# Rescheduling the transform stage of a hybrid encoder layer: query weights, output gates, Fourier output and row-0 corrections

## The chip, the cores and the metric

The kernel runs on one core of a Trainium2 chip. The metric is the device time of one execution in microseconds, median of three runs. All work is for that core: five engines with queues of their own (PE for matmuls, VectorE or DVE, ScalarE or ACT, GpSimd or POOL, SyncE or SP, which here only issues DMAs). Each engine takes its instructions strictly in the order that was fixed when the program was built.

## The reference

Two sequences of 1024 tokens and 1024 channels go through one encoder layer and a final norm, all in fp32. What matters for the change:

```python
mod = silu(c) @ w_ada + b_ada                  # six vectors: sh1, sc1, ga1, sh2, sc2, ga2
h = rmsnorm(x, g_mix) * (1 + sc1) + sh1
z = h @ w_in                                   # 256 q_lat | 128 kv_lat | 64 k_pe | 512 f_in
q = rmsnorm(q_lat, g_q_lat) @ w_uq             # 4 heads of 128 + 64 (the 64 with rope)
kv = rmsnorm(kv_lat, g_kv_lat) @ w_ukv         # keys and values of 4 heads
y_mla = softmax(q k^T / sqrt(192)) v           # 512 wide
fr = real(fft2(f_in, over tokens and within 8 groups of 64 channels, ortho))
y_four = fr @ w_four                           # per group, 512 wide
x = x + ga1 * (concat(y_mla, y_four) @ w_out)
h2 = rmsnorm(x, g_ffn) * (1 + sc2) + sh2
x = x + ga2 * ((silu(h2 @ w_gate) * (h2 @ w_up)) @ w_down)
y = rmsnorm(x, g_final)
```

## The kernel before

**Products.** An fp32 product is made from three matmuls of a rounded format (`mm3`, L79 to L81): high by high, high by low, low by high. `split` (L62 to L64) makes the two parts of an operand: a cast of the high part on ScalarE (L63) and a subtract for the low part on VectorE (L64). So every operand of a matmul costs one instruction on each of these engines, and the matmul waits for both. A matmul of 512 columns fills one PSUM bank.

**Stages.** (1) To about 234 us: modulation vectors, then eight "pairs" k = 0 to 7 (four of each sequence; two row blocks each): norm, transposes, the input projection `zproj` (L400), the latents of queries and keys (`latents`, with their own norm: squares on ScalarE at L411 and L412, a chain of six small GpSimd instructions at L102 to L109, scaling on VectorE at L423 and L424, transposes on PE at L438), and the first half of the Fourier transform. Since a real transform has a symmetry over tokens, `evenodd` (L386) makes sums and differences of mirrored blocks on GpSimd (L397), splits them, and `fourier_in` (L445) multiplies them by the channel-side matrices; the results are summed in `zc` (cosines), `zs` (sines) and a row-0 tile `zx`. While pair 7 runs, SP loads the tables `tcos`, `tsin`, `tcor` and the first of the folded weights into eight staging tiles of one tag (`raw_tile`).

(2) 234 to 332 us, the transform stage. For each sequence `dft` (L784) multiplies by the token-side tables: even rows of cosines into `pe`, odd rows into `po`, with a correction by `tcor` and the row-0 tile `zx` (L795) in `pe`. `prep_wm` (L821) loads and splits the folded weights (Fourier weights times output weights: `wm_d`, and `wn_d` for the Nyquist rows). `fourier_out` (L855) takes, for one row block j, both column halves g: 6 matmuls and one of the Nyquist rows into `pa`, 6 into `pb`, then sum and difference of the two give two mirrored row blocks, which SP stores to `fo_d`. For j = 0 there are 7 more (row 0). Between the row blocks of sequence 0 stand the second modulation's products (`mod2`). In sequence 1, `gate_wo` (L882) loads the output weights in eight tiles, multiplies them by the gate `ga1` on GpSimd (L896) and stores them to `wog_d` from GpSimd's queue (L897). `stage3_loads` (L707) loads what the attention of sequence 0 needs, one DMA chained behind the other: latents, the queries' latents, the raw query weights into staging tiles, the rope tables, the key latents; it splits the query weights. The first block's queries are then projected (`rope_q`, `absorb_q`, `rope_flip`) between the last row blocks of the Fourier output.

(3) 332 to about 790 us: attention in 64 items k (sequence, block of 256 queries, head, half). One item: scores on PE (L1050 to L1054), maximum (L1059), exponential (ACT L1064), scaling (L1066) on VectorE, transposes on PE (L1078), splits, values. Other work is hung on items by a table `todo` (from L1127): `wv_load` (L1110) loads the output weights (at k = 0 the gated ones from `wog_d` for sequence 0, at k = 34 and 35 the raw ones for sequence 1, which are then gated on GpSimd, L1118), `wv_split` (L1121) splits them, one tile an item for k = 3 to 10; the output projection begins at k = 11.

(4) 790 us to the end: the feed-forward block as seven products of quarter matrices, with sums of quarters on GpSimd and VectorE that are stored to and reloaded from DRAM (in the gate and up stage GpSimd stores at L1370 and L1384 to L1399), and the final norm.

**What sets the order.** The program is written in order, and a scheduler of the framework places each instruction in its engine's queue by that order and by its inputs. `issue_after(x)` and `first(a, b)` add an order between two instructions without a wait at run time, `behind()` puts splits after the last ones made.

The order in a pair and the loop over the Fourier output, in two lines each:

```python
fourier_in(k, 0); latents(k, 1); fourier_in(k, 1)      # in pair(k), L602 on
evenodd(k + 1, here["p"])
...
for s in range(2):
    for j in (1, 2, 3, 0):
        fourier_out(s, abn, j)                         # both halves g; s == 0: mod2 twice
```

## Time and profile before

| | us |
|---|---|
| median of 3 runs | 2078.36 |
| the runs | 2078.17, 2082.8, 2078.36 |
| the profiled execution | 2084.17 |
| its span in the profile | 2082.4 |
| busy: PE, VectorE, ScalarE, GpSimd | 2023.8, 1415.4, 896.3, 822.6 |

The span is the stretch from the first to the last recorded instruction; the execution's own time has 1.8 us around it. In the timeline a row gives start, duration, engine, line, operation, the tiles written and read, partitions and columns, and in brackets how long the engine had been idle before it and which instruction ended that. Matmuls overlap: their rows start one after the other more closely than their durations say, so a matmul's price is the distance of two starts. A row of the waits gives the waiting engine, line and tile, what it waited for, total, times and longest. The granted clock is the share of full speed at which PE was allowed to run.

### The profile page before, as it was taken

Reading aid. Unit: us, or ns where it says so; the run is one execution under the profiler, and the core shown is the slowest. Engines: PE = TensorE matmul, PEld = TensorE weight load, DVE = VectorE, ACT = ScalarE, POOL = GpSimd, SP = SyncE. Lnnn points to the kernel's source line nnn. Section 1 sums busy time; section 2 is a strip of 40 time slices with the busy share of each in tenths; the row PEclk is TensorE's granted clock in tenths of the full one; section 3 lists DMA queues with packets and bytes.
Section 4 is the critical chain, followed back from the end, with each engine's and each line's share of the span. In section 5 each row is a group of like instructions: output and inputs, shape, how many; then the busy total and the mean of one; then the engine's idle time right before and its main releaser. Section 6 shows DMA issues by size and latency. Waiting matters only on the chain.

```text
span 2082.4 us, 28692 instructions
## 1 busy us (share of the span) xinstructions
PE 2023.8 (97%) x9994; PEld 1658.4 (80%) x9994; DVE 1415.4 (68%) x2095; ACT 896.3 (43%) x1749; POOL 822.6 (40%) x1014
## 2 busy tenths in 40 slices
PE   7799989999999999999999999999999999999998
PEld 4688858888888887888888888887788888888876
DVE  4567757766676669777677666778665565566675
ACT  2655535555565555233332356454323323336441
POOL 0554211111312316778778610333554454420142
PEclk9999999999999999999999999999999999999999
DMA  9685685544553466546455488665332232258662
GB/s 389 201 255 166 223 314 204 132 102 92 146 122 112 160 220 219 173 174 205 164 177 200 159 267 269 213 233 185 112 118 101 82 121 102 77 172 282 227 230 94
DMA packets 184909, 374.56 MB, mean 180 GB/s; under 512 B 18716, under 2 KB 58524, under 8 KB 181692
## 3 DMA queue, kind: packets, MB, share of 16 engines
q1 hardware_dynamic: 166780, 317.14, 44.9%
q0 software_dynamic: 17984, 55.59, 8.9%
q8 instruction: 78, 1.28, 0.2%
q14 instruction: 67, 0.55, 0.1%
HBM read 258.56 MB, written 122.49 MB: 183 GB/s over the span
## 4 chain that ended last, share of the span: by engine, by line
PE 53%; DVE 3%; DMA 3%; POOL 1%; issue 1%; ACT 1%; SPq 0%; DVEq 0%; ACTq 0%; POOLq 0%
PE bank L81 18%; PE bank L80 18%; PE bank L79 17%; DVE wl L64 1%; DVE val L138 1%; DMA draw<-t_d 1%; DMA val<-x_d 1%; POOL val L138 1%; DMA draw<-s_d 1%; DMA draw<-in_w_down_dram 0%; ACT wh L63 0%; DVE val L1606 0%; DVE val L135 0%; DMA X<-hc_d 0%; DMA ga<-ga_d 0%
## 5 line engine op out<-in xcount | busy, mean ns | idle before, releaser
L81 PE MATMUL bank<-H,wl 128*128 128x512 f32 x1232 | 490.6, 398 | 0.2 <-DVE wl L64 0.2
L79 PE MATMUL bank<-H,wh 128*128 128x512 f32 x1232 | 483.8, 393 | 3.0 <-DVE val L138 1.1
L80 PE MATMUL bank<-H,wh 128*128 128x512 f32 x1232 | 486.1, 395 | 0.3 <-DVE H L64 0.3
L79 PEld LDWEIGHTS bank<-H,wh 128*128 128x128 f32 x1232 | 231.2, 188 | 60.4 <-DVE val L138 2.0
L80 PEld LDWEIGHTS bank<-H,wh 128*128 128x128 f32 x1232 | 231.3, 188 | 59.9 <-DVE H L64 0.6
L81 PEld LDWEIGHTS bank<-H,wl 128*128 128x128 f32 x1232 | 231.3, 188 | 53.9 <-DVE wl L64 0.5
L64 DVE TENSOR_TENSOR wl<-draw,wh 128x512 fp32r<-128x512 f32 x286 | 201.7, 739 | 83.9 <-ACT wh L63 83.3
L138 DVE TENSOR_TENSOR val<-bank,val 128x512 f32<-128x512 f32 x200 | 136.5, 688 | 157.2 <-PE bank L81 150.2
L63 ACT CAST wh<-draw 128x512 fp32r<-128x512 f32 x286 | 168.5, 619 | 158.6 <-PE bank L80 83.4
L138 POOL TENSOR_TENSOR val<-val 128x512 f32<-128x512 f32 x58 | 84.0, 1457 | 365.0 <-DVE val L1580 188.7
L80 PE MATMUL bank<-wl,wh 128*128 128x512 f32 x572 | 223.7, 391 | 2.2 <-DVE wl L64 2.2
L63 ACT CAST wh<-rgu 128x512 fp32r<-128x512 f32 x172 | 106.8, 621 | 270.1 <-PE bank L80 211.0
L81 PE MATMUL bank<-wh,wl 128*128 128x512 f32 x572 | 222.7, 389 | 0.0
L79 PE MATMUL bank<-wh 128*128 128x512 f32 x572 | 222.6, 389 | 0.0
L63 ACT CAST wh<-val 128x512 fp32r<-128x512 f32 x133 | 82.1, 620 | 268.7 <-PE bank L80 249.2
L64 DVE TENSOR_TENSOR wl<-val,wh 128x512 fp32r<-128x512 f32 x133 | 131.9, 994 | 76.1 <-ACT wh L63 76.0
L64 DVE TENSOR_TENSOR wl<-rgu,wh 128x512 fp32r<-128x512 f32 x172 | 166.8, 970 | 4.9 <-ACT wh L63 4.9
L135 POOL TENSOR_TENSOR val<-rgu 128x512 f32<-128x512 f32 x80 | 118.5, 1481 | 102.6 <-DMA rgu<-in_wgu_dram 88.3
L80 PEld LDWEIGHTS bank<-wl,wh 128*128 128x128 f32 x572 | 107.4, 188 | 28.1 <-DVE wl L64 5.8
L79 PEld LDWEIGHTS bank<-wh 128*128 128x128 f32 x572 | 107.4, 188 | 22.5
L81 PEld LDWEIGHTS bank<-wh,wl 128*128 128x128 f32 x572 | 107.4, 188 | 22.0
L1059 DVE TENSOR_REDUCE mx<-ps_s 128x1 f32<-128x1024 f32 x64 | 78.2, 1222 | 63.7 <-PE ps_s L1054 63.5
(352 smaller groups left out, 4113.6 us busy)
## 6 DMA issues: line engine op xcount, KB each, us to landing
rgu<-in_wgu_dram SPq DMA_DIRECT2D x86, 512.0 KB
draw<-s_d SPq DMA_DIRECT2D x143, 256.0 KB
s_d<-val POOLq DMA_DIRECT2D x88, 256.0 KB, 3.9
draw<-t_d SPq DMA_DIRECT2D x88, 256.0 KB
s_d<-val SPq DMA_DIRECT2D x66, 256.0 KB
draw<-in_w_down_dram SPq DMA_DIRECT2D x55, 256.0 KB
wada<-in_w_ada_dram SPq DMA_DIRECT2D x11, 1024.0 KB
xt<-in_x_dram SPq DMA_DIRECT2D x16, 512.0 KB
```

Of the source, the lines that this page charges most:

```text
L63: here["a"] = nc.scalar.copy(hi, src).ins
L64: here["v"] = nc.vector.tensor_tensor(out=lo, in0=src, in1=rd(hi), op=ALU.subtract).ins
L79: nc.tensor.matmul(out, lh, rh, start=first, stop=False, skip_group_check=cont)
L80: nc.tensor.matmul(out, lh, rl, start=False, stop=False, skip_group_check=cont)
L81: here["t"] = nc.tensor.matmul(out, ll, rh, start=False, stop=last, skip_group_check=cont).ins
L135: return eng.tensor_tensor(out=out, in0=x, in1=y, op=ALU.subtract).ins
L138: eng.tensor_tensor(out=out, in0=x, in1=y, op=ALU.add)
L1059: nc.vector.tensor_reduce(out=mx, in_=ps, axis=AX.X, op=ALU.max)
```

## The change

- **Odd halves.** The casts of the differences of pairs 2 to 7 are ordered behind the squares of that pair's first projection on ScalarE; GpSimd's products keep their place.
- **Row-0 copies** (three small ones a sequence) go from VectorE to ScalarE.
- **Ahead of pair 7** come the split of the row-0 tile, the cast of `tcor`, the split of the cosines of sequence 0 and the first quarter of the folded weights (rows 0 and 1, left half). SP's order there is `tcos`, `tsin`, `tcor`, weights.
- **`dft`:** the corrections follow the odd products. The zeroing of the Nyquist tile goes from VectorE to GpSimd.
- **Folded weights by column halves:** own tiles for each half; `fourier_out` takes one half, and a sequence runs through t = 0 to 7: all j of the left half, then all j of the right. One `mod2` a step. The Nyquist weights' subtract and scaling go from VectorE to GpSimd.
- **Query weights:** one DMA loads them raw into the tile of their low part during sequence 0, and they are split in place at t = 4 and 6 of sequence 0.
- **`stage3_loads`** loads the queries' latents and the rope tables only; latents and key latents are issued behind the stores of t = 0 to 3 of sequence 1. `rope_q` stands at t = 3, `absorb_q` and `rope_flip` at t = 5.
- **Output gates:** `gate_wo` and `wog_d` go. At k = 0 the raw output weights are loaded and the gates; the eight multiplies on GpSimd stand two an item at k = 4 to 7, the splits two an item at k = 6 to 9.
- **The program's space for GpSimd's DMA descriptors** is 8192 bytes (the framework's default is 16384).

```diff
@@ evenodd, zproj, fourier_in
+                    if i == 1 and k > 1:
+                        st1.setdefault(("odd", k), []).append(here["a"])
...
+            if u == 0:
+                for ins in st1.pop(("odd", k), ()):
+                    first(here["sq"], ins)
...
-                    nc.vector.tensor_copy(zx[0:1, NCOS * s : NCOS * s + NCOS], pc[0:1, :NCOS])
+                    nc.scalar.copy(zx[0:1, NCOS * s : NCOS * s + NCOS], pc[0:1, :NCOS])
@@ ahead of pair(nk - 1)
+        nc.sync.dma_start(cor[:, :NTE], a["tcor"])
+        nc.scalar.copy(tcor, cor[:, :NTE])
+        split(zxs[0], zxs[1], zx)
+        z0 = zcos_split(0)
+        def wm_half(s, g, h, pool):
+            wm = [pool.tile([P, 2, 512], F32R, tag=f"wm{i}{g}{h}", name=f"wm{i}{g}{h}", bufs=1) for i in range(2)]
+            for c in range(2):
+                raw = raw_tile("wraw")[:, :512]
+                here["wraw"] = nc.sync.dma_start(raw, wm_d[s][:, 2 * h + c, 512 * g : 512 * g + 512]).ins
+                if h == 0:
+                    split(wm[0][:, c, :], wm[1][:, c, :], raw)
...
+        wm0 = wm_half(0, 0, 0, wr)
         pair(nk - 1)
@@ stage3_loads
-        last = gate_wo(0, gate_after, None)
+        for i in range(2):
+            last = nc.sync.dma_start(rd(ql[i]), lat_d[0][i][:, 0:2, 0:256]).ins
...
-        for c in range(2):
-            then(wqr[c][1][:, :256], wq_d[:, c, 512:768])
-            then(wqr[c][0], wq_d[:, c, 0:512])
...
+        S["ld2"] = [(rd(lat[i]), lat_d[0][i][:, 2:4, :]) for i in range(2)] + [(rd(ckv[i]), ckv_d[0][i]) for i in range(2)]
@@ transform stage
-        here["ny"] = nc.vector.tensor_scalar(out=nyt, in0=raws[0, 0], scalar1=0.0, scalar2=None, op0=ALU.mult).ins
+        nc.gpsimd.tensor_scalar(out=nyt, in0=raws[0, 0], scalar1=0.0, scalar2=None, op0=ALU.mult)
...
-                for i in range(2):
-                    nc.tensor.matmul(pe[:m, :NTE], zxs[i][:, x0 : x0 + m], tcor, start=False, stop=i == 1)
                 for c in range(2):
                     mm3(po[:m, :256], zz[0][:, 2 * c + 1, :], zz[1][:, 2 * c + 1, :],
                         tb[0][0][:, c, NTE:NT], tb[0][1][:, c, NTE:NT], c == 0, c == 1)
+                for i in range(2):
+                    nc.tensor.matmul(pe[:m, :NTE], zxs[i][:, x0 : x0 + m], tcor, start=False, stop=i == 1)
...
+                nc.gpsimd.tensor_tensor(out=wnr, in0=wnr, in1=rd(wnh), op=ALU.subtract)
+                nc.gpsimd.tensor_scalar(out=wnr, in0=wnr, scalar1=cmask[:, 3 + 2 * s : 4 + 2 * s], scalar2=None, op0=ALU.mult)
...
+        nyq_split()
+        zsplit(0, z0)
+        nc.sync.dma_start(rd(wq_l), wq_d)
...
-            for j in (1, 2, 3, 0):
-                with tc.issue_after(S.pop("ld")) if (s, j) == (1, 1) else ExitStack():
-                    fourier_out(s, abn, j)
-                if (s, j) == (1, 1):
-                    gate_wo(1, None, here["st"])
+            for t in range(8):
+                with tc.issue_after(S["ld"]) if s == 1 and t < 2 else ExitStack():
+                    fourier_out(s, abn, (1, 2, 3, 0)[t % 4], t // 4)
+                if s == 1 and t < 4:
+                    with tc.issue_after(here["st"]):
+                        nc.sync.dma_start(*S["ld2"].pop(0))
...
+                    if t in (4, 6):
+                        c = t // 2 - 2
+                        with behind():
+                            split(wq_h[:, c, :], wq_l[:, c, :], rd(wq_l[:, c, :]))
@@ attention
-                nc.sync.dma_start(raw, (wog_d if s == 0 else wo_d)[:, h, gs])
+                nc.sync.dma_start(raw, wo_d[:, h, gs])
...
+        def wv_gate(i):
+            h, g = i % 4, i // 4
+            with tc.issue_after(here["p"]):
+                nc.gpsimd.tensor_tensor(out=S["wv", h, g], in0=S["wv", h, g], in1=S["ga"], op=ALU.mult)
...
-            todo[3 + i].append(lambda i=i: wv_split(i))
+            todo[(4, 4, 5, 5, 6, 6, 7, 7)[i]].append(lambda i=i: wv_gate(i))
+            if i == 3:
+                todo[5].append(lambda: gate_half(0, 1))
+            todo[6 + i // 2].append(lambda i=i: wv_split(i))
@@ program
-    nc = _bacc.Bacc("TRN2", target_bir_lowering=False, num_devices=1)
+    nc = _bacc.Bacc("TRN2", target_bir_lowering=False, num_devices=1, dynamic_dma_scratch_size=8192)
```

194 lines of the change are left out of this document (77 added, 117 removed).

## The prediction

> **What bounds the kernel now.** First the page's first part, for the engine that fills the span.
>
> ```profile
> span 2082.4 us, 28692 instructions
> ...
> PE   2023.8 (97%) x9994; PEld 1658.4 (80%) x9994; DVE 1415.4 (68%) x2095; ACT 896.3 (43%) x1749; POOL 822.6 (40%) x1014
> ```
>
> TensorE is busy for all but 58.6 us, and the change keeps its number of matmuls. So it can win only idle time of TensorE in the stages that it touches, and time in which TensorE ran at a lower clock. The waits of the transform stage (230 to 330 us) show the largest one and what stood behind it; the PE timeline shows its place.
>
> ```profile
> PE bank L79 <- ACT wq_h L63: 7.5, 1, 7.5
> ACT wq_h L63 <- DMA wqr<-wq_d: 5.5, 2, 5.2
> ```
> ```profile
> 290.65 0.48 PE L79 MATMUL bank<-wm,A 128*128 128x512 f32 x1
> ...
> 292.36 0.50 PE L79 MATMUL bank<-wm,B 128*128 128x512 f32 x1 [0.53 <-ACT wm L847]
> ...
> 311.45 0.80 PE L79 MATMUL bank<-wq_h,ql 128*128 128x256 f32 x2 [7.53 <-ACT wq_h L63]
> ...
> 330.78 0.40 PE L79 MATMUL bank<-wm,A 128*2 128x512 f32 x1
> ...
> 332.41 0.39 PE L1050 MATMUL ps_s<-lat,qa 128*128 128x512 f32 x1
> ```
>
> The query projection of the first attention block waits for weights that are loaded and split only then; the matmuls of the Fourier output stand behind it in PE's queue. The stretches by window (columns: us, then PE, PEld, DVE, ACT, POOL busy, granted clock, DMA share, GB/s) show what such gaps cost on top.
>
> ```profile
> 206.00:212.00 6.00, 4.17 (x22) 3.89 (x21) 3.68 (x9) 4.83 (x14) 4.37 (x11) 0.72 0.10 26
> 239.30:242.30 3.00, 2.99 (x14) 2.81 (x15) 2.42 (x5) 1.49 (x4) 0.00 (x0) 0.50 0.45 143
> 247.30:290.30 43.00, 43.00 (x237) 28.42 (x236) 25.24 (x45) 13.11 (x27) 1.58 (x3) 1.00 0.83 299
> 304.00:311.40 7.40, 0.00 (x0) 0.00 (x0) 3.46 (x6) 0.99 (x2) 1.01 (x2) 0.71 1.05 397
> 311.40:317.20 5.80, 5.75 (x19) 5.08 (x20) 4.16 (x11) 3.44 (x6) 1.41 (x2) 0.50 0.96 354
> ```
>
> After the 7.53 us gap the clock is 0.50 for 5.8 us, and it was 0.50 for 3.0 us after a gap of 1.88 us at 239.31 (below). Between the two, 247.3 to 290.3, PE is never idle: nothing is to be had there, only lost.
>
> **The change part by part.**
>
> **A, the query weights** (loaded whole into the low part's own tile during sequence 0 and split there; the gate products of the output weights, their loads and stores gone from this stage; Fourier output by column halves). From 290.65 to 332.41 the stretch has 118 matmuls of 512 columns (8 row-and-column blocks of 13, and two times 7 for row 0), 18 of 256 columns and 8 transposes. From 330.78 to 332.41 are 7 intervals: 0.233 us for 512 columns; 256 columns go at 0.12 (below); a transpose at 0.13 (8 in 1.06 us, row at 550.63 below). Full: 118 x 0.233 + 18 x 0.12 + 8 x 0.13 = 30.7 us, against 41.8. The loss of 11.1 is 7.53 + 0.53 + 2.9 (half of 5.8 us at clock 0.50) and 0.1 rest. Is something late in its place? The weights are split behind the fifth and seventh step of sequence 0, near 270 us, some 30 us ahead of use. The latents (2 MB) and the key latents (1 MB) now stand on SP behind the stores of the first four steps of sequence 1, that is from about 294 to 304 us; 3 MB at the 354 GB/s of the row above are 8.9 us, so by about 313 to 316, before the first score, which would then stand at 332.4 - 10.5 = 321.9. Credit 10.5 (the 0.53 wait on a weight half may stay); bounds 7.6 (the clock still drops somewhere) and 11.1.
>
> **B, the start of the transform** (row-0 corrections behind the odd products, cosine splits, row-0 splits and the first weight half done in the last pair, the zeroing of the Nyquist tile and the Nyquist weights' subtract and scale moved from VectorE to GpSimd).
>
> ```profile
> 234.57 0.28 PE L79 MATMUL bank<-tb,zh 128*128 128x258 f32 x1
> ...
> 235.85 0.39 PE L81 MATMUL bank<-tb,zh 128*128 128x258 f32 x1 [0.88 <-DVE zh L64]
> ...
> 239.31 0.58 PE L795 MATMUL bank<-tcor,zx 128*128 128x258 f32 x1 [1.88 <-DVE zx L64]
> ...
> 246.10 0.28 PE L81 MATMUL bank<-tb,zh 128*128 128x256 f32 x1
> ...
> 247.30 0.39 PE L79 MATMUL bank<-wm,A 128*128 128x512 f32 x1
> ```
>
> From 246.10 to 247.30 are 10 intervals, so 0.12 each; the 66 matmuls from 234.57 on would take 7.9 us and took 12.73. Both operands that came late are now made earlier, and the corrections come after six more matmuls (0.7 us). Of the 4.8 us, 0.88 + 1.88 + 1.5 (3.0 us at clock 0.50) = 4.3 goes. What may be late next: the Nyquist and sine splits, which now head VectorE's queue, and the Nyquist weights, wanted by the seventh matmul of the Fourier output (1.4 us after its start) behind two GpSimd passes. No trace shows these; bounds 3.5 and 4.8, I take 4.3, the two rows' own.
>
> **C, the odd halves' casts.** These are the rows of pair 6, on ScalarE, GpSimd and PE.
>
> ```profile
> 202.81 0.62 ACT L63 CAST eoh<-eo 128x512 fp32r<-128x512 f32 x1 [7.04 <-POOL eo L397]
> ...
> 204.59 0.38 ACT L411 ACTIVATE junk<-bank 128x256 bf16<-128x256 f32 x1
> ```
> ```profile
> 201.49 2.54 POOL L397 TENSOR_TENSOR eo<-hf 128x512 f32<-128x512 f32 x2 [5.03 <-DVE eol L64]
> 205.40 0.22 POOL L102 TENSOR_SCALAR rs_v<-mz 128x2 f32<-128x2 f32 x1 [1.37 <-ACT junk L412]
> ...
> 207.32 0.20 POOL L109 TENSOR_TENSOR rs_r<-rs_w,rs_y 128x2 f32<-128x2 f32 x1
> ```
> ```profile
> 208.09 1.06 PE L438 MATMUL bank<-ident,lat 128*128 128x128 f32 x4 [1.82 <-DVE lat L423]
> ```
>
> ScalarE stood 7.04 us in front of a cast whose input GpSimd had not made, and the squares of the latents' norm queued behind it. Now the squares go first (their projection ends near 200.6). GpSimd's order stays, so its norm chain (205.40 to 207.52, 2.1 us) starts when the two products let it, 203.2 to 204.0; the transposes follow its end by 0.57: 205.9 to 206.7, against PE ready at 206.27. The gap of 1.82 goes to 0 to 0.4, and with it the low clock up to 211.6 (3.5 us at half: 1.75). 3.57 in all; credit 3.3, bounds 2.8 and 3.6.
>
> **J, a new wait in the last pair.** The order of the instructions shows it: in VectorE's queue the subtracts of the first weight half (two, 0.69 each) now stand between the two normalisations of the latents of pair 7, in ScalarE's its two casts stand ahead of the next ones of the pair. They wait for weights that SP loads. Rows of before on VectorE, PE, SP, and the window:
>
> ```profile
> 225.99 0.34 DVE L424 TENSOR_SCALAR lat<-bank,rs_r 128x128 f32<-128x128 f32 x1
> ```
> ```profile
> 227.39 0.60 PE L438 MATMUL bank<-ident,lat 128*128 128x128 f32 x4
> ```
> ```profile
> 223.18 1.38 SPq L843 DMA_DIRECT2D wraw<-wm_d  x3
> ```
> ```profile
> 221.00:227.75 6.75, 6.75 (x37) 6.12 (x35) 2.56 (x8) 1.66 (x7) 2.28 (x8) 1.00 0.78 253
> ```
>
> By 227.75 the queue had moved 6.75 x 253 = 1.71 MB, which is the four tables, the correction and the two weight tiles (2 x 0.263 + 2 x 0.262 + 0.132 + 2 x 0.262). So the second tile is there at 227.75, is cast (0.62) and subtracted (0.69) by 229.05, and the normalisation, before at 225.99, ends at 229.4. PE is ready for its transposes at 227.39: a gap of 2.0, and 1.5 for the clock as after 1.88 above: 3.5. Bounds: 0.5 (tiles in order of issue and early) and 4.5 (the last byte at 228.6, as the queue shares its engines).
>
> In a sentence apart: the Trainium skill ("TensorE: Matmul & The Clock Gate", Part 1) lets the clock fall only after about 3.4 us idle; by that J would cost 2.0 and C and B would return 1.8 and 1.5 less. The trace differs, with 0.72 and 0.50 after gaps of 1.82 and 1.88.
>
> **E, output gates in the attention.** Eight GpSimd multiplies and, in items 6 to 9, two weight splits each where there was one in items 3 to 10. The same multiplies run already for sequence 1:
>
> ```profile
> 548.65 5.47 POOL L1118 TENSOR_TENSOR wvr<-wvr,gah 128x512 f32<-128x512 f32 x4 [4.30 <-DMA gah<-ga_d]
> ```
> ```profile
> 548.77 1.71 DVE L1066 TENSOR_SCALAR p<-p,rr 128x1024 f32<-128x1024 f32 x1
> ```
> ```profile
> 550.63 1.06 PE L1078 MATMUL ppt<-ident,p 128*128 128x128 f32 x8 [1.06 <-DVE p L1066]
> ```
> ```profile
> L1066 DVE TENSOR_SCALAR p<-p,rr 128x1024 f32<-128x1024 f32 x8 | 6.3, 792 | 0.2
> ...
> L64 DVE TENSOR_TENSOR wv<-wvr,wv 128x512 fp32r<-128x512 f32 x7 | 4.8, 680 | 0.0
> ```
> ```profile
> 345.00:385.00 40.00, 38.93 (x261) 34.55 (x260) 34.96 (x68) 25.24 (x49) 2.94 (x5) 1.00 0.32 70
> ```
>
> By the group rows of the stretch 345 to 385 us a scaling takes 0.79 and a split's subtract 0.68. Four multiplies cost PE 1.06 as the scaling went from 0.79 to 1.71 us. Eight: 2.1. The extra split in four items: VectorE is 87% busy (34.96 of 40), that is 4.5 us of a 5.15 us item, so 0.68 just fits; unhidden it is 2.7. Bounds 4.8 above, and -0.4 (waits of 0.18 and 0.19 at items with a split today). I take 1.0, half the multiplies' price: they are spread two to an item, behind another GpSimd add.
>
> In a sentence apart: the Trainium skill ("SBUF — State Buffer", "Who interferes with whom") has the pair of ports of VectorE and GpSimd locked for a whole instruction; by it eight of 1.37 us could stop VectorE for 10.9 us, and less the slack of 0.65 in four items PE would lose up to 8.3. The trace agrees in kind, with 0.92 us more on one scaling in four multiplies.
>
> **At nothing:** three one-row copies from VectorE to ScalarE (off PE's path; cover is the pair's matmuls, price without it under 1 us), and the halved space for GpSimd's DMA descriptors, of which no trace of before shows use (rival 4).
>
> **Sum:** -10.5 - 4.3 - 3.3 + 3.5 + 1.0 = **-13.6 us** on the profiled execution: 2084.17 to 2070.6. That execution lies 5.8 above the median of the runs (2078.36); from the median it is **2064.8**.
>
> **The rivals.**
>
> 1. *The weight tiles come early enough and J is not there* (its low bound less): -17.1, **2061.3**. For it: nothing else loads then. Against: 1.71 MB by 227.75.
>
> 2. *VectorE becomes the bound in items 4 to 9*: E at 4.5: **2068.3**. For it: 87% busy and the row at 548.77. Against: GpSimd's multiplies lie apart.
>
> 3. *The change doesn't do what it says:* another operand of the query block (latents, tables) or the weight halves comes late, and A's 10.5 stays in another form: -3.1, **2075.3**. For it: the DMA share of 0.96 to 1.05 in that stage. Against: eight loads and eight stores of 256 KB, those of the gated weights, are gone from it.
>
> 4. *Slower:* with half the descriptor space GpSimd waits at its DMA issues in the gate and up stage of the feed-forward block.
>
> ```profile
> 800.00:1190.00 390.00, 390.00 (x1672) 313.73 (x1673) 283.75 (x284) 123.24 (x210) 306.05 (x274) 1.00 0.53 182
> ```
> ```profile
> s_d<-val POOLq DMA_DIRECT2D x88, 256.0 KB, 3.9
> ```
> ```profile
> L1399 POOL DMA_DIRECT2D s_d<-val x40 | 22.1, 553 | 6.9 <-POOL val L135 3.0 <-POOL val L138 3.0 <-DVE wl L64 0.9
> ...
> L1388 POOL DMA_DIRECT2D t_d<-tdb x10 | 5.4, 539 | 0.0
> ```
>
> There it issues 96 transfers (six groups, first and last shown: 40, 16 and four of 10) in 390 us and has 84 us left: 0.87 each. Gain and slack are gone from 0.87 + 13.6/96 = 1.0 us more per transfer. If each waits half the 3.9 us to its landing: (1.95 - 0.87) x 96 = 104 less 13.6: **2168**. Against: a transfer every 4.1 us leaves about one outstanding.
>
> **How the numbers follow.** Chances: forecast 0.50, rival 1 0.16, rival 2 0.14, rival 3 0.12, rival 4 0.08. About 0.3% (6.2 us) is what a measurement of this kernel can tell from no change, so faster is below 2072.1: forecast, rivals 1 and 2, 0.80; within: rival 3, 0.12; slower: 0.08. The bounds that gain: A 0.6, B 0.5, C 0.3, J 3.0, E 1.4, 5.8 in all: 2059.0. Those that lose, A 2.9, B 0.8, C 0.5, J 1.0, E 3.8, would reach 2073.8; rival 3 lies at 2075.3. The range 2059.0 to 2075.5 holds all but rival 4 and the outer parts of the others.
>
> **What would show it.** A: no gap above 0.6 us ahead of the query matmuls, first score 30 to 32 us after the last transform matmul of sequence 1. B: 8 to 9 us from first transform matmul to first Fourier output. C: transposes of pair 6 without a gap, clock 1.00 there. J: a gap near 2.0 us at pair 7's first latent transposes, ended by VectorE, weight subtracts just ahead of it. E: PE idle in items 4 to 9 by about 1 us more. It is wrong if the transposes of pair 7 do not wait, if attention loses more than 4 us, or if PE shows waits on GpSimd after 790 us.

## The result, and the profile after

The changed kernel takes 2068.26 us (median of 6 runs, 2066.55 to 2074.12), the kernel before 2082.85 in the runs beside it (6 runs, 2078.17 to 2084.92). The ratio is 0.9939, interval 0.9921 to 0.9957: **0.6% faster, 12.7 us** (9.0 to 16.5 by the interval). Forecast were 2064.8 us and a gain of 13.6; the forecast time was counted from a median of three runs, 2078.36, and the same gain taken off 2082.85 would be 2069.2. The page's head:

```profile
span 2066.8 us, 28651 instructions
...
PE   2018.9 (98%) x9994; PEld 1652.4 (80%) x9994; DVE 1406.0 (68%) x2078; ACT 898.4 (43%) x1753; POOL 841.4 (41%) x1014
```

The PE timeline gives the places that the prediction named, in their order (in brackets: idle time ahead, and what ended it).

```profile
205.19 0.63 PE L442 MATMUL bank<-ident,lat 128*128 128x128 f32 x4 [0.46 <-DVE lat L427]
...
210.67 0.63 PE L442 MATMUL bank<-ident,lat 128*128 128x128 f32 x4 [0.87 <-DVE lat L427]
...
223.90 0.38 PE L442 MATMUL bank<-ident,lat 128*128 128x128 f32 x2
225.04 0.44 PE L442 MATMUL bank<-ident,lat 128*128 128x128 f32 x2 [0.76 <-DVE lat L428]
...
228.83 0.63 PE L442 MATMUL bank<-ident,lat 128*128 128x128 f32 x4 [0.25 <-DVE lat L427]
...
232.14 0.28 PE L79 MATMUL bank<-tb,zh 128*128 128x258 f32 x1
...
240.00 0.39 PE L79 MATMUL bank<-wm,A 128*128 128x512 f32 x1
...
242.20 0.50 PE L79 MATMUL bank<-wm,B 128*128 128x512 f32 x1 [0.65 <-ACT A L63]
...
243.88 0.50 PE L79 MATMUL bank<-wm,B 128*128 128x512 f32 x1 [0.32 <-ACT B L63]
...
246.68 0.50 PE L79 MATMUL bank<-wm,A 128*128 128x512 f32 x1
...
250.89 0.50 PE L79 MATMUL bank<-wm,A 128*128 128x512 f32 x1
...
279.36 0.39 PE L79 MATMUL bank<-tb,zh 128*128 128x258 f32 x1
...
286.01 0.48 PE L79 MATMUL bank<-wm,A 128*128 128x512 f32 x1
...
300.17 0.28 PE L79 MATMUL bank<-wq_h,ql 128*128 128x256 f32 x1
...
316.64 0.47 PE L1033 MATMUL ps_s<-lat,qa 128*128 128x512 f32 x1
```

The query matmuls at 300.17 have no bracket: the 7.53 us are gone. New are the brackets at 242.20 and 243.88, in a block where PE had none before. Cutting both timelines at the same instructions gives this table (us; each cell is the distance of two starts; "PE ready" is the start of pair 6's first latent transposes less the gap ahead of it):

| stretch | before | changed | difference | forecast |
|---|---|---|---|---|
| start to PE ready in pair 6 | 206.27 | 204.73 | -1.54 | 0 |
| to the first transform matmul (C, J) | 28.30 | 27.41 | -0.89 | +0.2 |
| to the first Fourier output (B) | 12.73 | 7.86 | -4.87 | -4.3 |
| to the second transform (output of sequence 0) | 36.66 | 39.36 | +2.70 | 0 |
| to sequence 1's Fourier output | 6.69 | 6.65 | 0 | 0 |
| to the first score (A) | 41.76 | 30.63 | -11.13 | -10.5 |
| to the first output product (E) | 58.27 | 59.30 | +1.03 | +1.0 |
| to the end | 1691.72 | 1690.86 | -0.86 | 0 |

The five differing middle rows sum to -13.2. The last row is in no part that the change edits. The first holds the odd casts of pairs 2 to 5, but the kernels with their new order (203.3 to 205.9) and without it (203.5 to 206.3) do not differ there. Over all profiles of this study the first row lies between 203.3 and 206.3, the last between 1689.0 and 1696.6. So a time tells 5 us apart here, hardly 1 us; the experiments on small waits are read from their stretches.

### The profile page after: what moved, and what is told of

Read it like the earlier page. It is cut to its first block, busy times and chain, and to the rows that moved or that the text cites. A ratio compares the mean times of both kernels' runs of the same rounds, so it can differ in the third digit from the quotient of the medians.

```text
span 2066.8 us, 28651 instructions
## 1 busy us (share of the span) xinstructions
PE 2018.9 (98%) x9994; PEld 1652.4 (80%) x9994; DVE 1406.0 (68%) x2078; ACT 898.4 (43%) x1753; POOL 841.4 (41%) x1014
## 4 chain that ended last, share of the span: by engine, by line
PE 55%; DVE 3%; DMA 2%; ACT 1%; POOL 1%; issue 1%; SPq 0%; DVEq 0%; ACTq 0%; POOLq 0%
PE bank L81 18%; PE bank L79 18%; PE bank L80 18%; DVE wl L64 1%; DMA draw<-t_d 1%; ACT wh L63 1%; DVE val L137 1%; DVE val L1599 0%; DMA val<-x_d 0%; DMA X<-hc_d 0%; DVE val L134 0%; DMA rgu<-in_wgu_dram 0%; DMA ga<-ga_d 0%; DMA draw<-s_d 0%; POOL rs_y L105 0%
```

## The experiments

Medians of 4 runs (e4 of 10, e6 of 7, e12 of 5) with their ratio to the kernel before, and the same stretches, each from one profile (us):

| run | time | ratio, interval | C, J | B | output 0 | transform 2 | A | E |
|---|---|---|---|---|---|---|---|---|
| e1 | 2068.61 | 0.9928 (0.9913 to 0.9943) | 28.10 | 7.86 | 39.21 | 6.65 | 30.63 | 59.29 |
| e2 | 2067.35 | 0.9924 (0.9909 to 0.9939) | 27.26 | 7.86 | 39.38 | 6.65 | 30.63 | 59.59 |
| e3 | 2071.51 | 0.9948 (0.9933 to 0.9963) | 28.08 | 7.86 | 38.32 | 6.65 | 32.94 | 59.37 |
| e4 | 2081.73 | 0.9995 (0.9986 to 1.0005) | 28.54 | 14.16 | 36.66 | 6.69 | 41.01 | 58.26 |
| e5 | 2070.26 | 0.9925 (0.9906 to 0.9944) | 26.89 | 7.86 | 40.59 | 6.64 | 30.60 | 59.25 |
| e6 | 2079.18 | 0.9975 (0.9964 to 0.9986) | 28.22 | 12.70 | 36.66 | 6.69 | 30.76 | 59.29 |
| e7 | 2071.78 | 0.9934 (0.9917 to 0.9951) | 26.91 | 7.86 | 37.04 | 7.92 | 31.59 | 59.38 |
| e8 | 2071.86 | 0.9937 (0.9921 to 0.9952) | 28.02 | 7.86 | 39.80 | 6.65 | 30.61 | 58.35 |
| e9 | 2071.15 | 0.9933 (0.9911 to 0.9954) | 27.56 | 7.86 | 37.17 | 7.85 | 32.23 | 59.36 |
| e10 | 2072.92 | 0.9943 (0.9926 to 0.9960) | 27.22 | 7.86 | 43.60 | 6.65 | 30.64 | 59.51 |
| e11 | 2072.88 | 0.9943 (0.9926 to 0.9960) | 27.12 | 7.86 | 42.28 | 7.85 | 32.03 | 59.24 |
| e12 | 2068.49 | 0.9929 (0.9915 to 0.9942) | 27.68 | 7.86 | 37.26 | 7.90 | 30.85 | 58.32 |

### What made the query weights late: e3 and e6

e3 is the changed kernel with the query weights loaded late again, but without the gate traffic.

```diff
-        nc.sync.dma_start(rd(wq_l), wq_d)
...
+        then(rd(wq_l), wq_d)
         then(rc, a["ropec"])
...
+                if s == 1 and t == 2:
+                    for c in range(2):
+                        with behind():
+                            split(wq_h[:, c, :], wq_l[:, c, :], rd(wq_l[:, c, :]))
```

> The changed kernel with the query weights loaded late: issued in sequence 1's stage right behind the queries' latents, as before the change, and split there behind the third step, ahead of the query matmuls. The gated output weights stay out of the stage. Theory 1: the early place of the load is what removed the wait of 7.5 us; then PE waits 4 to 8 us for the split again with the clock at 0.50 behind it, and the stretch from the first Fourier output of sequence 1 to the first score takes 37 to 42 us instead of 30.6: 7 to 11 us slower than the changed kernel. Theory 2: what stood in front of the query weights in the queue (1 MB of output weights, 2 MB of latents, the gated stores) made them late, and with that gone they land in time even from the late place; then the stretch stays within 1 us of 30.6 and the time the same as the changed kernel's.

e6 is the kernel before with the gating alone taken out of the stage.

```diff
-        last = gate_wo(0, gate_after, None)
+        last = None
...
-                if (s, j) == (1, 1):
-                    gate_wo(1, None, here["st"])
...
+            todo[(4, 4, 5, 5, 6, 6, 7, 7)[i]].append(lambda i=i: wv_gate(i))
+            todo[6 + i // 2].append(lambda i=i: wv_split(i))
```

> The kernel before with one part of the change: the gating of sequence 0's output weights, its eight loads and eight stores are out of the transform stage, and the multiplies and splits stand in the attention as in the changed kernel. The query weights are loaded as before, late and behind the latents, and all the rest is the kernel before. Theory 1: the traffic in front of the query weights made them late; the wait of 7.53 us falls to 0 to 4 us, the stretch from 290.65 to the first score (41.75 us) to 31 to 37, the attention to the first output product takes about 1 us more, and the time is 4 to 9 us below the kernel before. Theory 2: their late place behind 2 MB of latents is enough to make them late; the wait stays at 6 to 7.5 us and the time within 2 us of the kernel before.

PE timeline of e6, from the first Fourier output of sequence 1 to the first score:

```profile
288.81 0.48 PE L79 MATMUL bank<-wm,A 128*128 128x512 f32 x1
...
301.12 0.39 PE L79 MATMUL bank<-wq_h,ql 128*128 128x256 f32 x2
...
319.57 0.39 PE L1048 MATMUL ps_s<-lat,qa 128*128 128x512 f32 x1
```

No bracket at 301.12, though the loads of the query weights still stand behind the latents: 30.76 us, where the full rate gives 30.7 and the kernel before took 41.76. Theory 1 of e6 holds: the gated weights' loads and stores were the cause, and without them the late place of the query weights makes no wait. Only half of these transfers stood ahead of the query weights: the second four loads of the kernel before were issued at 313.48, behind the first cast of the query weights at 311.00. SP of the kernel before, then of e6:

```profile
293.07 2.85 SPq L894 DMA_DIRECT2D wor<-wo_d  x4
...
298.09 6.73 SPq L725 DMA_DIRECT2D wqr<-wq_d  x4
...
313.48 4.05 SPq L894 DMA_DIRECT2D wor<-wo_d  x4
```
```profile
291.52 5.51 SPq L725 DMA_DIRECT2D wqr<-wq_d  x4
```

Counted from the first Fourier output of sequence 1 (290.65 and 288.81), the first query load was issued 4.7 us later with the gating, and its data came at least 8.7 us later (the first cast starts at 311.00 and at 300.46). So one part is the place behind four loads in SP's queue, and another comes after the issue; no run separates the place from the bytes.

e3 has no wait at its query matmuls either, but its theory 2 holds only in part: its 32.94 lie 2.3 above the changed kernel, with short waits for the folded weights (0.26, 0.30 and 0.52) and one of 0.66 ahead of the first score. So the early load was not needed against the 7.53 us, but its place counts: sequence 0's Fourier output, the second transform and sequence 1's stage together take 76.64 us in the changed kernel and 77.91 in e3.

The ratio of e6 (0.9975, 5 us) is smaller than its stretches (-11.0 + 1.0); 4.9 us of the difference lie in the last stretch of its profile, where nothing was edited. What made that stretch longer was not found.

### The new wait in the first Fourier output: e1, e5, e9

The changed kernel's ScalarE and SP:

```profile
240.53 0.62 ACT L845 CAST wnh<-wnr 128x512 fp32r<-128x512 f32 x1 [2.53 <-DMA wnr<-wn_d]
```
```profile
232.86 0.60 SPq L879 DMA_DIRECT2D wq_l<-wq_d  x1
233.56 1.09 SPq L843 DMA_DIRECT2D wnr<-wn_d  x2
```

The Nyquist rows (98 KB a half) were issued at 233.56 and were there at 240.5. ScalarE waits for them with the casts of A and B behind it in its queue, and PE waits for those. Ahead of them in SP's queue stands the early query load, 786 KB.

e1 moves that line in the program:

```diff
-        nc.sync.dma_start(rd(wq_l), wq_d)
...
             prep_wm(0)
+        nc.sync.dma_start(rd(wq_l), wq_d)
```

> The changed kernel with one load moved: the raw query weights (786 KB) are issued on SP behind the Nyquist weights, the last folded-weight tile of the first quarter and the three small tables instead of ahead of them. In the changed kernel PE loses 2.7 us in the first block of the Fourier output of sequence 0 (from the first such matmul at 240.00 to the second block at 246.68: 6.7 us, where 13 + 8 matmuls of 0.233 would take 4.9 us and the small gaps of the modulation none). Theory 1: ScalarE stands 2.53 us in front of the cast of the Nyquist weights, whose load lies behind the query weights in SP's queue, and the splits of A and B queue behind that cast. Then the cast starts by about 238 us, the gaps of 0.65 and 0.32 us go, and the stretch from 240.00 to the second block takes 5.0 to 5.5 us: 1.2 to 2.0 us less, about 2066.5 us. Theory 2: the splits of A and B and the eight weight casts are more work than ScalarE and VectorE can do in that time; then the stretch stays above 6.2 us and the time the same.

e1 decides between neither theory: the scheduler put the load back in front of the Nyquist rows, the cast still waits 2.38 us, and the Fourier output takes 39.21 us. e5 orders the load instead:

```diff
         with tc.issue_after(here["wraw"]):
+            nc.sync.dma_start(rd(wq_l), wq_d)
             for c in range(3):
```

> The first trial of this left the load where it was in SP's queue: its row still stood ahead of the Nyquist weights. Here the load of the raw query weights is ordered behind the last folded-weight load of sequence 0's preparation, so that the Nyquist weights are issued first. Theory 1: the cast of the Nyquist weights on ScalarE no longer waits (2.53 us in the changed kernel), the gaps of 0.65, 0.32 and 0.16 us in the first block of the Fourier output go, and sequence 0's Fourier output, from its first matmul to the next transform, takes 38.1 to 38.5 us instead of 39.36, as in the trial with the late query weights (38.32). Theory 2: ScalarE and VectorE are simply behind with the splits; then it stays above 39.1 us.

The cast no longer waits, and the gaps of 0.65 and 0.32 are gone (0.17 is left). But the query load now stands ahead of the modulation's weights, and the same block waits for these, in e5:

```profile
245.46 1.93 PE L906 MATMUL bank<-wada,scT 128*32 128x512 f32 x8 [1.46 <-DMA wada<-in_w_ada_dram]
```

Behind that wait the clock was 0.50 for 3.4 us, in e5:

```profile
245.39:248.81 3.42, 3.35 (x12) 1.40 (x13) 0.58 (x1) 1.18 (x2) 3.29 (x2) 0.50 1.02 429
```

So the stage takes 40.59 us instead of 39.36. Theory 1 was right on the wait and wrong on the gain. e9 puts the load in the middle of the stage, behind the fourth step's stores, and the split into sequence 1.

```diff
+                    if t == 3:
+                        with tc.issue_after(here["st"]):
+                            nc.sync.dma_start(rd(wq_l), wq_d)
```

> The changed kernel with the query weights loaded in the middle: issued behind the stores of the fourth step of sequence 0's Fourier output and split in sequence 1 behind its third step. Of the two places tried, the early one makes the Nyquist weights late (sequence 0's stage 39.36 us, against 38.32 without it there), the one behind the first weights makes the modulation's chunk late (40.59, a wait of 1.46 us for it), and the late one costs 2.3 us in sequence 1's stage (32.94 against 30.63). Theory 1: it is the loads' order in a queue that is nearly full at the stage's start that decides; in the middle the load disturbs nothing: sequence 0's stage 38.2 to 38.6 us, sequence 1's 30.6 to 31.0, together with the transform between them 75.5 to 76.2 instead of 76.64. Theory 2: the three stages together are bound by the sum of their loads; what one wins the next gives back, and the sum stays at 76.5 to 78.

The three stages take 37.17 + 7.85 + 32.23 = 77.25 us (the modulation's last products lie behind the cut here, so only the sum compares): a wait of 0.89 for sequence 1's first weights and 0.25 for the query weights take the place of the earlier ones. The sum is that of theory 2: in each place tried, something behind the 786 KB in the queue is late. By these sums the changed kernel's early place is the best of the four, 76.64 against 77.91 (e3), 77.83 (e5) and 77.25 (e9); e1 and e2, which leave this part as it is, have 76.49 and 76.66.

### Twice as many changes of product: e7 and e12

```diff
-                    mod2(t)
+                    if t % 2 == 1:
+                        mod2(t - 1)
+                        mod2(t)
```

> The changed kernel with the second modulation's products called two chunks at every second step, as in the kernel before, instead of one at each. In the changed kernel sequence 0's Fourier output takes 39.36 us against 36.66 before; the trial with the late query weights took 38.32 without a wait for the Nyquist weights, so 1.66 us are left. Theory 1: each change between the 512-column products and the modulation's narrow ones costs about 0.2 us, and there are twice as many; with fewer changes the stage takes 38.3 to 38.9 us. Theory 2: the 1.66 us lie in the first block alone (splits of B, Nyquist weights); then the stage stays at 39.2 to 39.5.

Sequence 0's stage and the second transform together took 44.96 us instead of 46.01: 1.05 less. Nearly all of it, 0.98, lies in the first two blocks with their modulation, up to the start of the third: 10.89 us in the changed kernel (240.00 to 250.89), 9.91 in e7 (239.07 to 248.98). Two single chunks of modulation cost 0.33 more there than one pair: by the distance of starts, less two steps of 0.233, a single chunk takes 1.19 (249.56 to 251.22) and a pair 2.05 (270.44 to 272.96 in the kernel before). The other 0.65 goes with shorter waits in the first block, 0.42 and 0.32 us instead of 0.65, 0.32 and 0.16. So the changes are only a part of this gain, and each theory holds in part. Sequence 1's stage took 0.96 more, for this, in e7:

```profile
285.42 0.51 PE L80 MATMUL bank<-wm,A 128*128 128x512 f32 x1 [0.90 <-DVE wm L64]
```

e12 adds an earlier load of the first four weight tiles of sequence 1:

```diff
+                if s == 0 and t == 5:
+                    with tc.issue_after(here["st"]):
+                        for h in range(2):
+                            for c in range(2):
+                                raws[1, 0, h, c] = raw_tile("wraw")[:, :512]
+                                nc.sync.dma_start(raws[1, 0, h, c], wm_d[1][:, 2 * h + c, 0:512])
```

> The changed kernel with two edits: the modulation's products two chunks at every second step (in its own trial sequence 0's stage fell from 39.36 to 37.04 us, the transform behind it took 7.92 instead of 6.65, and sequence 1's stage waited 0.90 us for its first weights: 31.59 instead of 30.63), and the four weight tiles of sequence 1's left half loaded behind the stores of the sixth step of sequence 0. Theory 1: what the pairs win is given back because the next stage's weights are not there; with the four tiles loaded earlier the wait goes, and the three stages take 75.2 to 75.8 us instead of 76.64: about 1 us less than the changed kernel, which its time can't show but its stretches can. Theory 2: the three are bound by the sum of their loads; the earlier tiles take the place of the modulation's last chunk or of the stores, another wait comes, and the sum stays at 76.4 to 77.5.

The sum is 37.26 + 7.90 + 30.85 = 76.01, between the theories: 0.63 less than the changed kernel, with new waits of 0.35 (Nyquist weights) and 0.16 (modulation). Its time, 2068.49, is that of the changed kernel.

### Row blocks instead of column halves: e11

e11 is the kernel before with the gates moved, the odd casts, and the early row-0, correction and cosine splits; the Fourier output, the folded weights and the query weights are as before.

```diff
+        cor = raw_tile("raw")
+        nc.sync.dma_start(cor[:, :NTE], a["tcor"])
+        nc.scalar.copy(tcor, cor[:, :NTE])
+        split(zxs[0], zxs[1], zx)
+        z0 = zcos_split(0)
         pair(nk - 1)
```

> The kernel before with these parts of the change: the gates in the attention, the odd halves' casts behind the squares, the one-row copies on ScalarE, and the early row-0, correction and cosine splits with the corrections behind the odd products; the descriptor space is halved to make room. Not taken over: column halves of the Fourier output, the early first weight half, the early query weights, the Nyquist weights on GpSimd. With the gates alone moved, sequence 0's stage, the second transform and sequence 1's stage together took 74.1 us (85.1 before, 76.6 changed). Theory 1: the column halves cost 2.5 us and bring nothing; here the three take 74 to 75 us, the first transform 7.9 to 8.5, and the time is 1 to 3 us below the changed kernel. Theory 2: with the first transform 4.8 us shorter, the folded weights of both halves are late in the old order; PE waits 2 to 5 us in the first blocks of sequence 0, the three take 76.5 to 79 us, and the time is that of the changed kernel or above.

The first transform takes the same 7.86 us, but the three stages take 82.16. The first bracket is again the modulation's weights, in e11:

```profile
245.49 1.62 PE L940 MATMUL bank<-wada,scT 128*32 128x512 f32 x2 [2.19 <-DMA wada<-in_w_ada_dram]
```

Theory 2, and more than its 79 us: behind that wait the clock was 0.50 as well, for 3.4 us from 245.83. Step B takes 4.9 us off the transform in both kernels, and the Fourier output then starts ahead of its loads. With row blocks 8.05 us come back against e6's 74.11; in the changed kernel 2.53. So what e11 leaves out, the column halves and the early weight half, the early query load and the Nyquist weights on GpSimd, lets B keep half of its gain; of these four only the query load was tried apart (e3, e5, e9).

### Odd casts: e8

```diff
-            if u == 0:
-                for ins in st1.pop(("odd", k), ()):
-                    first(here["sq"], ins)
```

> The changed kernel without the order of the odd halves' casts behind the squares; all else as changed. Theory 1: ScalarE stands again in front of the cast of GpSimd's difference, the squares of pair 6's first projection start after it, PE waits 1.5 to 2.0 us at the transposes of the latents with a clock between 0.5 and 0.75 behind it, and the stretch from PE ready there to the first transform matmul takes 29 to 30.5 us instead of 27.4: about 2 us slower than the changed kernel. Theory 2: the gap was bound by GpSimd's norm chain behind its own products, which kept their place; then the gap stays below 1 us and the stretch within 0.5 us of 27.4.

The gap is back (1.66 us), as theory 1 has it, but the clock stayed at 1.00 and the stretch is only 0.61 longer than in the changed kernel. In the kernels without the order the gap was 1.82, 2.14, 2.25 and 1.66; with it 0.46, 1.16, 0.31, 1.13, none, none, 0.59, 0.56, none and 0.60: about 1.5 us less on average. Of the 1.20 us by which e8's gap is longer, half does not arrive, because the last pair loses less: from its first to its second latent transposes e8 takes 4.36 us (223.81 to 228.17), with one wait of 0.67, and the changed kernel 4.93.

### Later weight tiles: e10

```diff
+        with tc.issue_after(here["cor"]):
+            here["dd"] = nc.sync.dma_start(dd, a["w_ada"][0:P, 0:1024]).ins
+        with tc.issue_after(here["dd"]):
+            wm0 = wm_half(0, 0, 0, wr)
```

> The changed kernel with 0.5 MB of other data (a copy from DRAM to DRAM that nothing reads) in SP's queue ahead of the first folded-weight tiles, and with the order of the changed kernel on VectorE and ScalarE held by hand: the subtracts of the weight half between the two normalisations of the latents of pair 7. It tests the prediction's step J with the delay that the changed kernel did not have: there the loads started about 3 us earlier than forecast and PE waited 0.76 us. Theory 1: the tiles land 2 to 4 us later, PE waits 2 to 4.5 us at the first latent transposes of pair 7, and the granted clock there falls to 0.5 to 0.75 for about 3 us, so that the stretch from PE ready at pair 6's latents to the first transform matmul takes 30.5 to 33 us instead of 27.4. Theory 2 (the Trainium skill's rule that the clock falls only after about 3.4 us idle): the same wait, but with the clock at 1.00 behind it as long as the wait is below 3.4 us; the stretch grows by the wait alone.

The wait of 2 to 4.5 us, which both theories need, did not come: PE waited 0.91 us in pair 7 instead of 0.76. The first tile's cast started 0.28 us ahead of the pair's first latent transposes (224.77 against 225.05), in the changed kernel 1.65 ahead (222.25 against 223.90), so the tiles were only 1.4 us later; and PE's order had six Fourier matmuls moved ahead of the late transposes, which covered 0.9 us. What the extra 0.5 MB did is in the Fourier output, 4.24 us longer, with waits of 1.78 and 1.90 us for splits and weights. The price of a wait of 2 to 4 us in pair 7 was thus not tried.

### Gates apart, and the descriptor space: e2 and e4

```diff
+            p = S["p", *items[k]]
+            place = nc.gpsimd.tensor_tensor(out=pc, in0=p[:, 0:1], in1=p[:, 0:1], op=ALU.add).ins
+            with tc.issue_after(place):
...
+            todo[2 + i].append(lambda i=i: wv_gate(i, 2 + i))
+            todo[3 + i].append(lambda i=i: wv_split(i))
```

> The changed kernel with the eight gate multiplies on GpSimd one an item (2 to 9), each held until that item's scaling on VectorE is done (by a one-column add that reads the scaled tile), and the splits one an item (3 to 10) as in the kernel before. In the changed kernel the multiplies ran as two rows of four (333.8 and 342.7 us), a scaling took 1.67 us inside the second, and PE waited 0.95 us; from the first score to the first output product it took 59.30 us against 58.27 before. Theory 1: a multiply that runs while VectorE scales is what costs the 1.0 us. Then no scaling in items 2 to 10 is over 1.0 us, the wait of 0.95 goes, and the stretch takes 58.2 to 58.5 us: 0.8 to 1.1 us less. Theory 2: the price is that of eight more instructions and of splits bunched two an item; then the stretch stays at 59.0 to 59.5 us with the multiplies apart, or falls with no change of the scalings.

The scalings stayed at 0.74 to 0.76 us but for one (1.23), and the stretch did not fall: 59.59. PE's wait of 0.95 fell to 0.32, and new ones of 0.25, 0.44 and 0.19 us came. The multiply now met the splits. From e2, VectorE and GpSimd:

```profile
340.35 1.81 DVE L64 TENSOR_TENSOR wv<-wvr,wv 128x512 fp32r<-128x512 f32 x1
```
```profile
340.32 1.29 POOL L1110 TENSOR_TENSOR wvr<-wvr,gah 128x512 f32<-128x512 f32 x1
```

A subtract of 0.68 us alone took 1.81 beside a multiply that began 0.03 us ahead of it. Only one part of theory 1 stands: the collision is the price, but here it came with a subtract that reads two SBUF tiles.

e4 is the kernel before with the halved descriptor space.

```diff
-    nc = _bacc.Bacc("TRN2", target_bir_lowering=False, num_devices=1)
+    nc = _bacc.Bacc("TRN2", target_bir_lowering=False, num_devices=1, dynamic_dma_scratch_size=8192)
```

> The kernel before with one thing changed: the space for GpSimd's DMA descriptors is 8192 bytes instead of 16384. All the rest is the kernel before. Theory 1: GpSimd has about one transfer outstanding, so the space is never short; the time is the kernel's before within 0.2%, and in the gate and up stage its stores still take about 0.55 us to issue. Theory 2 (the prediction's rival 4): GpSimd waits at its issues; its stores there take over 1 us, and the time is above that of the kernel before.

0.9995 (0.9986 to 1.0005), and the issue of a store in the gate and up stage takes the same 553 ns:

```profile
L1399 POOL DMA_DIRECT2D s_d<-val x40 | 22.1, 553 | 5.9 <-POOL val L138 3.0 <-POOL val L135 3.0
```

The halving makes room for the changed kernel's larger set of staging tiles; it costs nothing that these runs can tell.

## Why the prediction was right, point by point

**A** was right in size (11.1 against 10.5): the wait, the 2.9 us charged to the low clock behind it and the 0.53 all went. Its mechanism was too wide: it credited early weights and removed traffic together. In the kernel before, e6 gives the whole to the traffic. The early load delays what stands behind it by about 1 us, and the three other places tried cost 0.6 to 1.3 us more in sum.

**B** was right for the transform (4.87 against 4.3, 7.86 us in every kernel that has it) and wrong in what it is worth. The step that failed is the sentence on what may be late next: it named the Nyquist weights and took nothing for them. 2.70 us came back in the next stage. Of it, 1.97 lies in the first two blocks with their modulation, 10.89 us in the changed kernel against 8.92 before (247.30 to this row of the kernel before):

```profile
256.22 0.50 PE L79 MATMUL bank<-wm,A 128*128 128x512 f32 x1
```

The other 0.7 lies behind them, where no bracket stands and the modulation's chunks come one by one. Of the 1.97, about 1 us is the Nyquist wait behind the query load (38.32 in e3, where the cast doesn't wait) and 0.33 the first two single chunks. Together the single chunks thus account for about 1 us, which the prediction did not count at all; this is read from the rows and not shown by a run of its own. The remaining 0.6 is not resolved. Behind the Nyquist wait lies the queue: this stretch of the changed kernel, in its window,

```profile
242.00:246.70 4.70, 3.90 (x16) 1.33 (x16) 4.43 (x8) 4.70 (x11) 2.71 (x4) 1.00 1.02 424
```

moves 424 GB/s with the DMA engines full. Here about half of the time won ahead of the full queue was paid back behind it.

**C** was half right. The gap went from 1.82 to 0.46 and the clock stayed at 1.00, as forecast. Not foreseen was the gap of 0.87 us in the same pair at full clock (210.67), which the kernel before does not have: at half clock the norm chain had time to finish. From the first latent transposes of pair 6 to the second it is 6.09 us before (208.09 to this row) and 5.48 in the changed kernel (205.19 to 210.67):

```profile
214.18 0.60 PE L438 MATMUL bank<-ident,lat 128*128 128x128 f32 x4
```

So the 1.75 us credited for the clock came to 0.6, and C in all to 2.0 instead of 3.3.

**J** failed, by the moment at which the loads start. The wait is there and is what it was said to be: the second normalisation (L428) behind the two subtracts, 0.76 us. From the first to the second latent transposes of pair 7 it is 4.93 us (223.90 to 228.83) against 3.86 before (227.39 to 231.25), so J cost 1.1. Forecast were a wait of 2.0 and a lower clock, 3.5 in all, from the landing of the tiles in the kernel before. But there the first table load stood waiting for GpSimd, and in the changed kernel it does not. SP's waits and its first load before, the second transposes of pair 7 before, and SP and ScalarE after:

```profile
SPq L626 <- POOL eo L397: 2.6, 1, 2.6
```
```profile
220.90 0.82 SPq L626 DMA_DIRECT2D raw<-in_tcos_dram  x2
```
```profile
231.25 0.63 PE L438 MATMUL bank<-ident,lat 128*128 128x128 f32 x4 [0.17 <-DVE lat L423]
```
```profile
215.30 1.11 SPq L630 DMA_DIRECT2D raw<-in_tcos_dram  x2
```
```profile
222.25 1.28 ACT L63 CAST wm<-wraw 128x512 fp32r<-128x512 f32 x2 [0.26 <-DMA wraw<-wm_d]
```

Before, the loads were issued from 220.90, 6.5 us ahead of the latent transposes at 227.39; after, from 215.30, 8.6 us ahead of those at 223.90. Rival 1 was the nearer one here; the wait of a load for the buffer it fills had not been read.

**E** was right at 1.03, but the figure was a choice between 0 and 1. The second four multiplies start 3.2 to 3.6 us after the issue of the gates' second half; in e8 the row names that load as what they waited for, in the changed kernel PE's transposes. Where the scaling of that item begins just after a multiply, it takes 1.67 us and PE waits 0.95; where it begins just before one, it takes 0.76 and PE does not wait. The changed kernel and e8, GpSimd and then VectorE of each:

```profile
342.73 5.49 POOL L1107 TENSOR_TENSOR wvr<-wvr,gah 128x512 f32<-128x512 f32 x4 [3.24 <-PE ppt L1061]
```
```profile
344.18 1.67 DVE L1049 TENSOR_SCALAR p<-p,rr 128x1024 f32<-128x1024 f32 x1
```
```profile
342.82 5.49 POOL L1104 TENSOR_TENSOR wvr<-wvr,gah 128x512 f32<-128x512 f32 x4 [3.58 <-DMA gah<-ga_d]
```
```profile
343.91 0.76 DVE L1046 TENSOR_SCALAR p<-p,rr 128x1024 f32<-128x1024 f32 x1
```

A quarter of a microsecond between the two engines decides: 59.30 us in the one, 58.35 in the other, and 58.32 in e12. The forecast's bunching was wrong as well (the multiplies ran four in a row, not two an item), and the splits two an item cost nothing: those kernels have one PE wait of 0.19 at that place, as before. In e8 it is the multiply behind the scaling that is longer, 1.74 us (from 344.08) against 1.30 for the one ahead of it. By the Trainium skill ("SBUF — State Buffer", "Who interferes with whom") the later one to issue waits for the whole instruction of the other; the rows agree in kind, with 0.9 and 1.1 us more on VectorE (1.67 against 0.76 here, 1.81 against 0.68 in e2) and 0.4 on GpSimd.

**Rival 4** is answered by e4. The sum, -13.6 against -13.2 in the touched stretches, is so close by luck, since its misses cancel: C gave 1.3 us less than forecast and the 2.7 that came back behind B were missing, while J was charged 2.4 too much and A and B gave 0.6 each more.

## What to carry to other kernels

When a stage's transfers keep the queues full, count a saved wait only after asking which load the next instruction needs and what stands ahead of it in the queue: here, against 4.9 us saved, 1.9 (e12) to 8 us (e11) came back in the next three stages, depending on the order of the loads. To find out which of two bundled edits works, make each alone: in the kernel before, taking out the gated weights' transfers did all of step A without the early load. And a landing time read from the old trace holds only while the load's own wait for its buffer stays the same.

## What the runs showed of the hardware that was not expected

The granted clock does not follow from a gap's length alone. The same transposes of pair 6 found these gaps and clocks (windows of 3 us behind the gap of 1.82 us in the kernel before, and behind that of 2.25 us in e6):

```profile
208.10:211.10 3.00, 3.00 (x14) 2.98 (x15) 2.32 (x6) 2.75 (x9) 1.95 (x3) 0.52 0.18 47
```
```profile
206.80:209.80 3.00, 3.00 (x25) 2.94 (x26) 2.32 (x6) 2.75 (x9) 1.98 (x3) 1.00 0.18 48
```

The longer gap kept the full clock; so did 1.66 us in e8, while 2.14 us in e4 fell to 0.50. In e10 two waits close together, 1.78 and 1.90 us, brought 0.50:

```profile
246.60:249.50 2.90, 2.90 (x10) 1.88 (x14) 2.90 (x5) 2.87 (x6) 1.00 (x3) 0.50 0.99 415
```

Single gaps up to 1.16 us never did in these stretches; e5's of 1.46 did. What sets this apart is where the gaps lie. In the kernel before, the falls start at 208.19, 238.91 and 307.18 us, 9 and 20 steps of 3.413 us apart, and last one, one and three such steps. The step ahead of a fall and the step of the fall, in the kernel before and in e5, and two steps of e6 on the same grid (ten steps ahead of its own fall at 236.99), show how much of a step PE was busy:

```profile
204.78:208.19 3.41, 1.58 (x9) 1.14 (x8) 1.63 (x6) 2.40 (x8) 2.25 (x8) 1.00 0.01 2
208.19:211.60 3.41, 3.41 (x17) 3.39 (x18) 2.73 (x8) 3.25 (x10) 2.31 (x4) 0.50 0.17 43
```
```profile
241.98:245.39 3.41, 1.81 (x6) 0.71 (x4) 3.41 (x7) 3.39 (x7) 1.73 (x2) 1.00 0.99 410
```
```profile
202.86:206.27 3.41, 1.67 (x9) 1.21 (x7) 1.49 (x6) 3.03 (x9) 1.70 (x6) 1.00 0.11 34
206.27:209.68 3.41, 2.89 (x24) 2.83 (x25) 2.73 (x6) 2.62 (x9) 2.33 (x4) 1.00 0.16 44
```

The 1.82 us of the kernel before lie in one step, the 2.25 us of e6 in two. Over all profiles of this study, between 200 and 320 us, PE was busy for 0.15 to 1.81 us of the step ahead of each fall, and for 1.67 us and more of every step that kept the full clock, so the edge is near half a step and no sharper in these rows. The Trainium skill ("TensorE: Matmul & The Clock Gate", Part 1) has a window of about 3.4 us that runs free of the program; the rows agree with that, but not with the page's whole idle window, since about half of one was enough. And the low clock cost less than its half rate: without its gap, the stretch from PE ready to the transform is 26.48 us before and 26.40 in e4 with it, 25.97 in e6 without, which is 0.4 to 0.5 us for 3.4 us at half clock, since at full clock PE waits 0.89 us for the next latents instead.
